# A decoder trunk with split-float32 products: the low part of every third MLP weight tile by an accumulating DMA

## The chip, the cores and the metric

One Trainium2 chip, of which the kernel uses one core. The metric is the time of one execution in device microseconds, the median of the runs shown.

## The reference

The input is x, 256 tokens of 2048 features in float32. Layer 0 is a gated mixer, layer 1 sliding-window attention, and behind each stands an MLP with squared ReLU; every sublayer is followed by a layer norm of alpha times the residual plus its output. What matters here are the two MLPs:

```python
def sq_relu_mlp(x, w_up, w_down):
    return jnp.square(jax.nn.relu(x @ w_up)) @ w_down

# in reference(), for each of the two layers
        x = layer_norm(DEEPNORM_ALPHA * x + mix, ln_g[layer, 0], ln_b[layer, 0])
        x = layer_norm(DEEPNORM_ALPHA * x + sq_relu_mlp(x, mlp_w_up[layer], mlp_w_down[layer]),
                       ln_g[layer, 1], ln_b[layer, 1])
```

w_up is [2048, 8192] and w_down is [8192, 2048], so each MLP reads 128 MiB of weights.

## The kernel before

Every matrix product is done with float32r operands, to float32 accuracy: each operand is a high part (the value rounded to float32r) and a low part (what is left), and a product is the sum of three: high by high, high by low, low by high. All weights of the program stand in one list, in the order of their use, as tiles [128, 1024] of float32, 512 KB each. An MLP has 256 of them (128 of w_up, 128 of w_down): for each quarter of the hidden features 32 tiles of w_up and then 32 of w_down.

The class Weights carries a tile through three stages.

- load() (line 107) and dma() (line 117): SP issues the load of a tile into one of RAW = 4 raw slots, w_raw (line 119). The loads keep the order of the program, so one that waits for its slot holds back all that are behind it.
- ahead() (line 83): a tile that has a place for its parts is split. ScalarE copies raw to w_hi, which rounds it (line 95); VectorE subtracts w_hi from raw and gives w_lo (line 97). Both read the raw slot, and it is free for the load of the tile four further on when both are done. In part of the layer-1 query projection GpSimd does some of the subtractions (by_pool, line 163).
- get() (line 121) and release() (line 130): the products take a tile, and when they are done its place is free. There are SLOTS = 5 places for parts, and EXTRA_SLOTS = 5 more are lent for the time of each MLP (lend(), line 62), ten in all. get() of a tile splits as many tiles ahead as there are places.

The split of a tile and the load behind it are written where a place comes free, so ScalarE, VectorE and SP each follow TensorE through the ring of places. The products are rows_product (line 210: activations stationary, weights moving, 12 matmuls of 512 columns a tile, lines 205 to 207; w_lo is the moving operand of the second of each three) for w_down, and cols_product (weights stationary, lines 246 and 251; w_lo in line 251) for w_up. ScalarE and VectorE also evict the products: in w_up after each four tiles, in w_down after each eight.

A scheduler orders the instructions of each engine by their readiness and adds the semaphore waits; TensorE, ScalarE, VectorE, GpSimd and SP each work through their own list in order.

Of the kernel before, what the change touches and what calls it, by code (L numbers as in the profile page):

```python
# [14 lines left out]
ALU = mybir.AluOpType  # L15
# [16 lines left out]
NEG = -3.0e38  # L32
# [15 lines left out]
class Weights:  # L48
    """The weights in the order of their use: each tile [128, 1024] is loaded and split
    into two float32r parts (high + low = the float32 value) ahead of its products."""  # L50

    def __init__(self, tc, pool, tiles):
        self.tc, self.nc, self.pool, self.tiles = tc, tc.nc, pool, tiles
        self.others, self.by_pool = [], ()
        self.borrowed, self.borrowed_from = [], 0
        self.raw, self.parts, self.held = {}, {}, []
        self.n_raw = self.n_split = self.n_used = 0
        self.free = {"w": SLOTS, "extra": 0}
        self.extra, self.extra_end = None, 0
        self.in_order = False  # L60

    def lend(self, pool, end):
        """More places for the parts of the tiles before number `end`."""
        self.extra, self.extra_end = pool, end
        self.free["extra"] = EXTRA_SLOTS

    def borrow(self, tile, first):
        """Room for the parts of a few tiles from number `first` on, once each."""
        self.borrowed, self.borrowed_from = [(tile[:, i, 0], tile[:, i, 1]) for i in range(4)], first
# [13 lines left out]
    def ahead(self, n_split=None):  # L83
        """Split the tiles that have a place, and load the ones after them."""
        nc = self.nc
        n_split = len(self.tiles) if n_split is None else n_split
        while self.n_split < min(n_split, len(self.tiles)):
            place = self._place(self.n_split)
            if place is None:
                break  # L90
            kind, hi, lo = place
            self.load(self.n_split + 1)
            raw = self.raw.pop(self.n_split)
            for s in self.pieces(self.n_split):
                nc.scalar.copy(out=hi[:, s], in_=raw[:, s])  # L95
                engine = nc.gpsimd if self.n_split in self.by_pool else nc.vector
                sub = engine.tensor_tensor(out=lo[:, s], in0=raw[:, s], in1=hi[:, s].bitcast(F32),  # L97
                                           op=ALU.subtract)
                if self.in_order:
                    self.tc.keep_in_program_order(sub)  # L100
            self.parts[self.n_split] = (hi, lo, kind)
            self.n_split += 1
    def pieces(self, n):
        """The first tile goes in halves, so that the products start early."""
        return [slice(0, TILE // 2), slice(TILE // 2, TILE)] if n == 0 else [slice(0, TILE)]
# [11 lines left out]
    def dma(self, out, in_):  # L117
        """Loads keep the order of the program: what is used first is loaded first."""
        self.tc.keep_in_program_order(self.nc.sync.dma_start(out=out, in_=in_))
# [10 lines left out]
    def release(self):  # L130
        """The oldest tile in use has been used."""
        kind = self.held.pop(0)
        if kind != "borrowed":
            self.free[kind] += 1
# [3 lines left out]
def trunk(ctx: ExitStack, tc: tile.TileContext, t, out):  # L138
    nc = tc.nc
# [13 lines left out]
    ends = {}  # L153
    for name in ("win_v", "win_u", "wout", "mlp0", "kv", "wq", "wo", "mlp1"):
        tiles = (mlp_order(tiles_of("up" + name[3:]), tiles_of("down" + name[3:]))
                 if name.startswith("mlp") else tiles_of(name))
        if name == "wo":
            # the last heads' rows of the first two chunks come after the other rows of both
            tiles = tiles[0:6] + tiles[8:14] + tiles[6:8] + tiles[14:]
# [3 lines left out]
    weights.by_pool = range(ends["kv"] + 4, ends["wq"], POOL_EVERY)  # L163
# [1 line left out]
    ident = const.tile([P, P], F32, name="ident")  # L165
# [21 lines left out]

# [1 line left out]
    def row_steps(stat, apart=False):  # L189
        """[tokens, 512] of both token tiles: activations stationary, weights moving.  # L190
        One step for each weight tile and token tile."""
        if apart:
# [26 lines left out]
    def col_steps(stat, merged=False):  # L219
        """Two blocks [128 features, 256 tokens], transposed: weights stationary. Columns  # L220
        256.. hold the part of the activations' low halves, unless it is merged into the others.
        One step for each weight tile, of both token tiles (tok None); or two, the first with
        the high parts' products of token tile 0."""
        ps = psum.tile([P, 2, 2 * S], F32, tag="mm", name="ps_c")

        def step(i, tok, hi, lo):
            for j in range(4):
                k = 4 * i + j
                for b in range(2):
# [3 lines left out]
                    def high():  # L233
                        if tok is not None:
                            # token tile 0 opens the bank for both
                            part, x = (a.rearrange("p (h t) -> p h t", h=2)[:, :, tok * P:(tok + 1) * P]
# [33 lines left out]
    def skewed(steps, lead, done=None, turn_at=()):  # L270
        """The steps of token tile 0 run `lead` weight tiles ahead of tile 1's; after the
        steps of turn_at, a part of the transposes of a layer norm."""
        held = []
# [16 lines left out]
    def gather_halves(ps, bias=None):  # L290
        """The sum of the two column halves of cols_product (with a bias per feature)."""
        part = work.tile([P, 2, S], F32, tag="part", name="part")
# [9 lines left out]

# [1 line left out]
    def stats_tile():  # L304
# [11 lines left out]
    def norm_rows(acc, stats, g, b, tok, done):  # L316
        """acc = the layer norm of acc, by column chunks; done(chunk) follows each."""
        mu, rstd = moments(stats, tok)
# [18 lines left out]
    def norm_transposed(acc, stats, g, b, xT, tok):  # L337
        """acc = the layer norm of acc, and its transpose goes to xT in parts."""
        def turn(q):
# [9 lines left out]
    def residual(acc, ps, n, stats, scale, toks=range(NT)):  # L349
        """acc = scale * acc + ps on column chunk n."""  # L350
        s = slice(n * 512, (n + 1) * 512)
# [6 lines left out]
    def last_rows(x, stat, stats, scale, norm, norm_turns=True):  # L358
        """The last column chunk before a layer norm: the norm of token tile 0 runs while
        the products of tile 1 do."""  # L360
        ps, steps = row_steps(stat, apart=True)
# [12 lines left out]
    def mlp(x, xT, norm, loads, tags, end):  # L374
        """norm(stats, hT, tok) follows the products of a token tile."""
        stats = stats_tile()
# [32 lines left out]

# [1 line left out]
    cos = const.tile([P, S], F32, name="cos")  # L411
# [4 lines left out]
    sink = const.tile([P, NQH], F32, name="sink")  # L416
    # 0 where key j of the band [previous block | own block] is seen by query i, else NEG
    mask = const.tile([P, 2 * P], F32, name="mask")
# [5 lines left out]

# [1 line left out]
    x = big.tile([P, NT, D], F32, tag="xa", name="x")  # L426
# [107 lines left out]

# [1 line left out]
    with tc.tile_pool(name="attn", bufs=2) as attn:  # L536
# [17 lines left out]

        # keys, transposed, each head's high and low parts in both halves of the partitions;
        # values by rows
        psk, steps = col_steps(xT)
# [18 lines left out]
        for h in range(2):  # L576
            src = kr[h * HD:(h + 1) * HD]
            for other in (h, 1 - h):
# [7 lines left out]
                                in1=bvv.unsqueeze(1).to_broadcast([P, NT, NKV * HD]), op=ALU.add)  # L586
        # [keys, block, kv head, high | low part]
        vp = attn.tile([P, NT, NKV, 2 * HD], F32R, bufs=1, name="vp")
# [4 lines left out]
        def attention(g, qT):  # L593
            """The steps of kv head g: (block of queries, heads, key blocks) at a time."""
            units = [(0, 0, 8, 1), (1, 0, 4, 2), (1, 4, 4, 2)]
# [49 lines left out]
            def values(u):  # L645
                n, h0, nh, nb = units[u]
                pT = st["pT", u].rearrange("p a (r j b) q -> p a r j b q", r=2, b=nb)
                w = nh // 2 * P
                # both parts of the values of the even heads, then of the odd ones
                ps = psum.tile([P, 2, 512], F32, tag="aux", name="ps_o")  # L650
# [31 lines left out]
        for g in range(NKV):  # L682
            # the high and the low parts of a head are 64 partitions each
            qT = attn.tile([P, QPK, S], F32R, tag="qT", bufs=1, name="qT")
# [56 lines left out]
def row_tiles(w):  # L741
    """[K, N] -> [N / 512 * K / 256, 128, 2 * 512]: two K tiles of 512 columns."""
    k, n = w.shape
    return w.reshape(k // 256, 2, P, n // 512, 512).transpose(3, 0, 2, 1, 4).reshape(-1, P, TILE)


def col_tiles(w):
    """[K, N] -> [N / 256 * K / 512, 128, 4 * 256]: four K tiles of 256 columns."""
    k, n = w.shape
# [56 lines left out]
```

## Time and profile before

| | |
|---|---|
| median of 2 runs | 2009.91 us (2007.93 and 2011.89) |
| span of the profiled execution | 2008.3 us |
| TensorE (PE) busy | 1963.9 us, 98% of the span |
| VectorE (DVE) busy | 1252.5 us, 62% |
| ScalarE (ACT) busy | 915.5 us, 46% |
| GpSimd (POOL) busy | 103.1 us, 5% |
| moved by DMA | 377.54 MB |

The profile is of one execution. It gives the span from the first to the last instruction; of what lies around the span it shows nothing, and the runs beside it are from 0.4 us below the span to 3.6 above it. The first MLP lies between about 260 and 970 us of the span, the second between about 1260 and 1960. Busy time of TensorE is from pipelined matmuls whose ends are modelled, so its busy share says that work was always at hand, not how fast it went.

### The profile page before, as it was taken

How to read it: one execution, taken by the hardware profiler on the slowest of the kernel's cores; microseconds unless marked ns; L12 is line 12 of the kernel's file. 1: busy time of each engine (PE TensorE's matmuls, PEld its weight loads, DVE VectorE, ACT ScalarE, POOL GpSimd, SP SyncE). 2: the span in 40 equal slices, each digit the busy share in tenths (PEclk: the TensorE clock that was granted, in tenths of full speed). 3: DMA queues.
4: the chain of work that ended last, by engine and by line, in shares of the span. 5: the costliest groups of instructions: out<-in, count | busy, mean ns of one | idle time of the engine just before them, and what ended most of it. 6: DMA issues, size and time to landing. Idle time of an engine off the chain costs nothing.

```text
span 2008.3 us, 26243 instructions
## 1 busy us (share of the span) xinstructions
PE 1963.9 (98%) x10388; PEld 1685.8 (84%) x10388; DVE 1252.5 (62%) x1345; ACT 915.5 (46%) x1138; POOL 103.1 (5%) x63
## 2 busy tenths in 40 slices
PE   9999999999999999999998889999999999999997
PEld 7888888888888888888898878888888888888886
DVE  5676686555554655564778997965555555555555
ACT  5445445434443443443456675444344344434432
POOL 0000010000000000000133310100000000000001
PEclk9999999999999999999998899999999999999999
DMA  9754846666666666655543336566676666665653
GB/s 339 259 186 151 301 143 214 189 197 224 192 192 191 187 189 194 190 184 166 179 137 107 104 106 227 175 208 190 197 228 187 194 189 189 189 194 185 189 157 104
DMA packets 105963, 377.54 MB, mean 188 GB/s; under 512 B 12272, under 2 KB 12912, under 8 KB 105840
## 3 DMA queue, kind: packets, MB, share of 16 engines
q1 hardware_dynamic: 105840, 375.86, 59.4%
q8 instruction: 81, 1.33, 0.3%
q14 instruction: 42, 0.34, 0.0%
HBM read 373.72 MB, written 2.10 MB: 187 GB/s over the span
## 4 chain that ended last, share of the span: by engine, by line
issue 82%; PE 8%; DVE 6%; ACT 2%; POOL 2%; DMA 0%; SPq 0%; POOLq 0%; ACTq 0%; DVEq 0%
PE ps_r L205 2%; PE ps_r L206 2%; PE ps_r L207 2%; DVE w_lo L97 1%; ACT p L623 1%; PE ps_c L242 1%; PE ps_c L251 1%; DVE x L332 0%; DVE swap L544 0%; POOL rstd L313 0%; DVE pT L186 0%; POOL x L328 0%; POOL x L327 0%; DVE qT L697 0%; DVE x L330 0%
## 5 line engine op out<-in xcount | busy, mean ns | idle before, releaser
L97 DVE TENSOR_TENSOR w_lo<-w_raw,w_hi 128x1024 fp32r<-128x1024 f32 (+1 forms) x655 | 803.9, 1231 | 569.7 <-ACT w_hi L95 567.7
L95 ACT CAST w_hi<-w_raw 128x1024 fp32r<-128x1024 f32 (+1 forms) x669 | 701.3, 1051 | 760.3 <-PE ps_r L207 413.4
L205 PE MATMUL ps_r<-w_hi,hT 128*128 128x512 f32 x1024 | 398.5, 389 | 0.0
L207 PE MATMUL ps_r<-w_hi,hT 128*128 128x512 f32 x1024 | 398.5, 389 | 0.0
L206 PE MATMUL ps_r<-w_lo,hT 128*128 128x512 f32 x1024 | 398.4, 389 | 0.0
L246 PE MATMUL ps_c<-yT,w_hi 128*128 128x512 f32 x960 | 337.1, 398 | 0.0
L246 PE MATMUL ps_c<-oT,w_hi 128*128 128x512 f32 x960 | 337.1, 398 | 0.0
L251 PE MATMUL ps_c<-yT,w_lo 128*128 128x256 f32 x992 | 272.5, 281 | 0.0
L251 PE MATMUL ps_c<-oT,w_lo 128*128 128x256 f32 x992 | 272.5, 281 | 0.0
L207 PEld LDWEIGHTS ps_r<-w_hi,hT 128*128 128x128 f32 x1024 | 192.2, 188 | 40.0
L206 PEld LDWEIGHTS ps_r<-w_lo,hT 128*128 128x128 f32 x1024 | 192.2, 188 | 40.0
L205 PEld LDWEIGHTS ps_r<-w_hi,hT 128*128 128x128 f32 x1024 | 192.2, 188 | 39.5
L246 PEld LDWEIGHTS ps_c<-oT,w_hi 128*128 128x128 f32 x960 | 178.7, 188 | 41.8
L246 PEld LDWEIGHTS ps_c<-yT,w_hi 128*128 128x128 f32 x960 | 178.7, 188 | 41.8
L251 PEld LDWEIGHTS ps_c<-yT,w_lo 128*128 128x128 f32 x992 | 187.4, 189 | 2.7
L251 PEld LDWEIGHTS ps_c<-oT,w_lo 128*128 128x128 f32 x992 | 187.4, 189 | 2.7
L300 DVE TENSOR_TENSOR full<-ps_c,part 128x512 f32<-128x512 f32 x73 | 50.5, 691 | 91.5 <-ACT part L294 83.7
L294 ACT COPY part<-ps_c 128x512 f32<-128x512 f32 x72 | 42.2, 587 | 131.2 <-PE ps_c L246 128.5
L242 PE MATMUL ps_c<-hT,w_hi 128*128 128x256 f32 x512 | 97.8, 294 | 0.0
L313 POOL TENSOR_TENSOR rstd<-ve,half 128x1 f32<-128x1 f32 x10 | 9.9, 987 | 1709.1 <-DVE ve L311 1709.1
L246 PE MATMUL ps_c<-xT,w_hi 128*128 128x512 f32 x256 | 90.2, 396 | 0.0
L242 PEld LDWEIGHTS ps_c<-hT,w_hi 128*128 128x128 f32 x512 | 84.4, 203 | 0.4
(141 smaller groups left out, 2026.4 us busy)
## 6 DMA issues: line engine op xcount, KB each, us to landing
w_raw<-in_up SPq DMA_DIRECT2D x256, 512.0 KB, 4.2
w_raw<-in_down SPq DMA_DIRECT2D x256, 512.0 KB, 4.1
w_raw<-in_win_u SPq DMA_DIRECT2D x32, 512.0 KB, 4.0
w_raw<-in_wout SPq DMA_DIRECT2D x32, 512.0 KB, 4.4
w_raw<-in_wq SPq DMA_DIRECT2D x32, 512.0 KB, 3.6
w_raw<-in_wo SPq DMA_DIRECT2D x32, 512.0 KB, 4.0
w_raw<-in_win_v SPq DMA_DIRECT2D x31, 512.0 KB, 6.2
b_ln_g<-in_ln_g SPq DMA_DIRECT2D x8, 512.0 KB, 5.6
```

What stands on the lines that cost most here:

```text
L95: nc.scalar.copy(out=hi[:, s], in_=raw[:, s])
L97: sub = engine.tensor_tensor(out=lo[:, s], in0=raw[:, s], in1=hi[:, s].bitcast(F32), op=ALU.subtract)
L205: nc.tensor.matmul(out=ps[tok], lhsT=xh, rhs=wh, start=first, stop=False)
L206: nc.tensor.matmul(out=ps[tok], lhsT=xh, rhs=wl, start=False, stop=False)
L207: nc.tensor.matmul(out=ps[tok], lhsT=xl, rhs=wh, start=False, stop=last)
L242: nc.tensor.matmul(out=ps[:, b, 0:S], lhsT=hi[:, w], rhs=stat[:, k, h * S:(h + 1) * S], start=first and h == 0, stop=last and h == 1)
L246: nc.tensor.matmul(out=ps[:, b, :], lhsT=hi[:, w], rhs=stat[:, k, :], start=first, stop=last)
L251: nc.tensor.matmul(out=ps[:, b, 0:S], lhsT=lo[:, w], rhs=stat[:, k, 0:S], start=False, stop=False)
L294: nc.scalar.copy(out=part, in_=ps[:, :, S:])
L300: nc.vector.tensor_tensor(out=full, in0=ps[:, :, 0:S], in1=part, op=ALU.add)
L313: nc.gpsimd.tensor_tensor(out=rstd, in0=ve, in1=half, op=ALU.pow)
L623: nc.scalar.activation(out=p[:, i, :], in_=p[:, i, :], func=AF.Exp, bias=top[:, i:i + 1], accum_out=den[:, i:i + 1])
```

## The change

A set by_dma names every third tile of each MLP, but for the first 40 and the last 40: 59 tiles of each, 118 in all. For these, ScalarE writes the negated value of raw, rounded to float32r, to w_lo (that is minus the high part), and a DMA issued by GpSimd adds the raw tile onto it; the sum is the low part. The VectorE subtraction of these tiles is gone. Comments and docstrings are taken out too, which moves line numbers by six.

```diff
-        self.others, self.by_pool = [], ()
+        self.others, self.by_pool, self.by_dma = [], (), ()
...
             for s in self.pieces(self.n_split):
                 nc.scalar.copy(out=hi[:, s], in_=raw[:, s])
+                if self.n_split in self.by_dma:
+                    nc.scalar.mul(out=lo[:, s], in_=raw[:, s], mul=-1.0)
+                    nc.gpsimd.dma_start(out=lo[:, s], in_=raw[:, s], accum_op=ALU.add)
+                    continue
                 engine = nc.gpsimd if self.n_split in self.by_pool else nc.vector
                 sub = engine.tensor_tensor(out=lo[:, s], in0=raw[:, s], in1=hi[:, s].bitcast(F32),
                                            op=ALU.subtract)
...
     weights.by_pool = range(ends["kv"] + 4, ends["wq"], POOL_EVERY)
+    weights.by_dma = (set(range(ends["wout"] + 40, ends["mlp0"] - 40, 3))
+                      | set(range(ends["wo"] + 40, ends["mlp1"] - 40, 3)))
```

Three places show what moves. The numbers behind a name tell one buffer from the next; DMAHW, DMASW, DVE, PE and Activation in a wait are the semaphores of loads, of DMAs from GpSimd, and of the engines. The first is SP's queue of loads where the range begins, before:

```order
L119 DMA w_raw_3201<-in_down0 128x1024 [waits DMAHW2_49,DVE_49]
L119 DMA w_raw_3223<-in_down0 128x1024 [waits DMAHW3_49,DVE_49]
L119 DMA w_raw_3253<-in_down0 128x1024 [waits DMAHW4_49,DVE_49]
L119 DMA w_raw_3271<-in_down0 128x1024 [waits DMAHW5_49,DVE_49]
L119 DMA w_raw_3289<-in_down0 128x1024 [waits DMAHW6_49,DVE_49]
L119 DMA w_raw_3307<-in_down0 128x1024 [waits DMAHW7_49,DVE_49]
L119 DMA w_raw_3325<-in_down0 128x1024 [waits DMAHW0_49,DVE_49]
L119 DMA w_raw_3343<-in_down0 128x1024 [waits DMAHW1_49,DVE_49]
```

and the same eight loads now:

```order
L123 DMA w_raw_3201<-in_down0 128x1024 [waits DMAHW2_49,DVE_49]
L123 DMA w_raw_3224<-in_down0 128x1024 [waits DMAHW3_49,DMASW0_49,Activation_49]
L123 DMA w_raw_3254<-in_down0 128x1024 [waits DMAHW4_49,DVE_49]
L123 DMA w_raw_3272<-in_down0 128x1024 [waits DMAHW5_49,DVE_49]
L123 DMA w_raw_3291<-in_down0 128x1024 [waits DMAHW6_49,DMASW1_49,Activation_49]
L123 DMA w_raw_3309<-in_down0 128x1024 [waits DMAHW7_49,DVE_49]
L123 DMA w_raw_3327<-in_down0 128x1024 [waits DMAHW0_49,DVE_49]
L123 DMA w_raw_3346<-in_down0 128x1024 [waits DMAHW1_49,DMASW2_49,Activation_49]
```

Every third load waits for an accumulating DMA (DMASW) in the place of a VectorE subtraction. The second place is ScalarE in the same part of the program, before:

```order
L95 CAST w_hi_3267<-w_raw_3179 128x1024 [waits DMAHW5_49,PE_49]
L95 CAST w_hi_3285<-w_raw_3201 128x1024 [waits DMAHW6_49,PE_49,Activation_49]
L95 CAST w_hi_3303<-w_raw_3223 128x1024 [waits DMAHW7_49,PE_49,Activation_49]
L95 CAST w_hi_3321<-w_raw_3253 128x1024 [waits DMAHW0_49,PE_49,Activation_49]
L95 CAST w_hi_3339<-w_raw_3271 128x1024 [waits DMAHW1_49,PE_49,Activation_49]
L95 CAST w_hi_3357<-w_raw_3289 128x1024 [waits DMAHW2_49,PE_49,Activation_49]
```

and now:

```order
L95 CAST w_hi_3268<-w_raw_3179 128x1024 [waits DMAHW5_49,PE_49]
L97 ACTIVATE w_lo_3287<-w_raw_3201 128x1024 [waits DMAHW6_49,PE_49]
L95 CAST w_hi_3286<-w_raw_3201 128x1024 [waits PE_49,Activation_49]
L95 CAST w_hi_3305<-w_raw_3224 128x1024 [waits DMAHW7_49,PE_49,Activation_49]
L95 CAST w_hi_3323<-w_raw_3254 128x1024 [waits DMAHW0_49,PE_49,Activation_49]
L97 ACTIVATE w_lo_3342<-w_raw_3272 128x1024 [waits DMAHW1_49,PE_49]
L95 CAST w_hi_3341<-w_raw_3272 128x1024 [waits PE_49,Activation_49]
```

The negation (ACTIVATE) of every third tile stands ahead of the cast of the same tile, not behind it as in the code. The third place is TensorE at the first tile of the range, before:

```order
L205 MATMUL ps_r_3395<-w_hi_3219,hT_2655 128x512 [waits PE_49]
L206 MATMUL ps_r_3395<-w_lo_3220,hT_2655 128x512
L207 MATMUL ps_r_3395<-w_hi_3219,hT_2655 128x512
L205 MATMUL ps_r_3395<-w_hi_3219,hT_2655 128x512
L206 MATMUL ps_r_3395<-w_lo_3220,hT_2655 128x512
```

and now:

```order
L211 MATMUL ps_r_3398<-w_hi_3219,hT_2655 128x512 [waits PE_49]
L212 MATMUL ps_r_3398<-w_lo_3220,hT_2655 128x512 [waits DMASW0_49]
L213 MATMUL ps_r_3398<-w_hi_3219,hT_2655 128x512
L211 MATMUL ps_r_3398<-w_hi_3219,hT_2655 128x512
L212 MATMUL ps_r_3398<-w_lo_3220,hT_2655 128x512
```

TensorE's order is the same; its first product with the low part waits for the accumulating DMA.

## Rows read from the trace of the kernel before

**Rows 1.** The page: span, and busy time of each engine.

```profile
span 2008.3 us, 26243 instructions
PE 1963.9 (98%) x10388; PEld 1685.8 (84%) x10388; DVE 1252.5 (62%) x1345; ACT 915.5 (46%) x1138; POOL 103.1 (5%) x63
```

**Rows 2.** Busy time by stretches, two of each MLP; columns in the first row.

```profile
core 0: us, PE busy (x) PEld busy (x) DVE busy (x) ACT busy (x) POOL busy (x), PEclk, DMA share, GB/s
500.00:600.00 100.00, 100.00 (x510) 84.90 (x509) 56.31 (x56) 43.15 (x47) 0.00 (x0) 1.00 0.64 190
600.00:700.00 100.00, 100.00 (x517) 85.24 (x516) 55.25 (x55) 43.28 (x47) 0.00 (x0) 1.00 0.63 190
1600.00:1700.00 100.00, 100.00 (x516) 85.19 (x515) 54.46 (x54) 42.70 (x45) 0.00 (x0) 1.00 0.63 190
```

**Rows 3.** Who waited for whom, 300 to 900 us: us, times, longest.

```profile
DVE w_lo L97 <- ACT w_hi L95: 218.6, 144, 1.9
ACT w_hi L95 <- PE ps_r L207: 154.9, 93, 1.7
ACT w_hi L95 <- PE ps_c L246: 105.5, 60, 1.8
...
ACT w_hi L95 <- DMA w_raw<-in_up: 1.4, 1, 1.4
```

**Rows 4.** Timeline of ScalarE: start, us, instruction, idle before it.

```profile
599.50 1.05 ACT L95 CAST w_hi<-w_raw 128x1024 fp32r<-128x1024 f32 x1 [1.66 <-PE ps_r L207]
602.22 1.05 ACT L95 CAST w_hi<-w_raw 128x1024 fp32r<-128x1024 f32 x1 [1.67 <-PE ps_r L207]
```

**Rows 5.** Timeline of VectorE, same stretch.

```profile
597.98 1.22 DVE L97 TENSOR_TENSOR w_lo<-w_raw,w_hi 128x1024 fp32r<-128x1024 f32 x1
600.59 1.23 DVE L97 TENSOR_TENSOR w_lo<-w_raw,w_hi 128x1024 fp32r<-128x1024 f32 x1 [1.39 <-ACT w_hi L95]
```

**Rows 6.** What SP's queue waited for, 300 to 900 us.

```profile
SPq L119 <- DVE w_lo L97: 505.6, 217, 3.5
```

**Rows 7.** DMA queues and issues, 300 to 900 us; the last number is us to landing.

```profile
q1 hardware_dynamic: 32143, 117.00, 64.0%
...
w_raw<-in_up SPq DMA_DIRECT2D x112, 512.0 KB, 4.2
w_raw<-in_down SPq DMA_DIRECT2D x105, 512.0 KB, 4.2
b_ln_g<-in_ln_g SPq DMA_DIRECT2D x2, 512.0 KB, 5.7
b_ln_b<-in_ln_b SPq DMA_DIRECT2D x2, 512.0 KB, 5.4
```

**Rows 8.** Groups by line, 320 to 860 us: busy us, mean ns, idle before.

```profile
L97 DVE TENSOR_TENSOR w_lo<-w_raw,w_hi 128x1024 fp32r<-128x1024 f32 x195 | 238.6, 1224 | 204.0 <-ACT w_hi L95 203.7
L95 ACT CAST w_hi<-w_raw 128x1024 fp32r<-128x1024 f32 x195 | 205.3, 1053 | 248.0 <-PE ps_r L207 154.9 <-PE ps_c L246 88.7 <-PE ps_c L251 4.1
```

**Rows 9.** All loads of line 119, whole span.

```profile
DMA to landing us min/median/max: 2.6/4.2/10.3
```

**Rows 10.** DMA issues of the page; the last number is us to landing.

```profile
w_raw<-in_down SPq DMA_DIRECT2D x256, 512.0 KB, 4.1
...
w_raw<-in_win_v SPq DMA_DIRECT2D x31, 512.0 KB, 6.2
...
lnv_b<-in_lnv_b SPq DMA_DIRECT2D x2, 512.0 KB, 8.9
```

**Rows 11.** Timeline of TensorE in the stretch of rows 4 and 5.

```profile
599.30 0.39 PE L205 MATMUL ps_r<-w_hi,hT 128*128 128x512 f32 x1
599.53 0.39 PE L206 MATMUL ps_r<-w_lo,hT 128*128 128x512 f32 x1
599.75 0.39 PE L207 MATMUL ps_r<-w_hi,hT 128*128 128x512 f32 x1
...
600.89 0.39 PE L206 MATMUL ps_r<-w_lo,hT 128*128 128x512 f32 x1
601.12 0.39 PE L207 MATMUL ps_r<-w_hi,hT 128*128 128x512 f32 x1
601.34 0.39 PE L205 MATMUL ps_r<-w_hi,hT 128*128 128x512 f32 x1
```

## The prediction

> **What bounds the kernel now.** I read the page first, then the busy times by stretches, then who waits for whom in a stretch, and last the timelines of single engines. The page shows TensorE busy for 1963.9 of 2008.3 us, VectorE for 62%, ScalarE for 46%, GpSimd for 5% [rows 1]. The stretches say where the missing 44 us are not: inside both MLPs TensorE is busy 100.00 of 100 us, at a granted clock of 1.00, that is the 2.4 GHz level, and GpSimd executes nothing [rows 2]. So in the stretch that the change touches nothing but TensorE's own pace can be won, and every wait that reaches TensorE is a loss.
>
> The waits of 300 to 900 us, which lie in the first MLP, show the direction: VectorE waits for ScalarE (218.6 us) and ScalarE waits for TensorE (154.9 and 105.5 us), because a split starts when TensorE gives a place back. No TensorE row stands among them, and ScalarE waited for a weight load once, for 1.4 us [rows 3]. ScalarE casts one tile every 2.72 us after 1.67 us of idling [rows 4], and VectorE subtracts 1.23 us right behind [rows 5]. SP waits for that subtraction before nearly every load, 217 times, 505.6 us in all [rows 6]: the raw slot is the only thing that holds a load back. 217 loads in 600 us make 2.765 us a tile.
>
> A load needs 4.2 us from issue to landing [rows 7]. The raw slot comes round after four tiles, 11.1 us; cast, subtraction and load use 1.05 + 1.22 + 4.2 = 6.5 of them [rows 7, 8]. The spare time is 4.6 us a tile. For the finished parts there are ten places, so a part is needed nine tiles, 24.9 us, after its place came free.
>
> **Removed.** 118 subtractions of 1.224 us [rows 8], 144 us of VectorE. No TensorE row waits for VectorE there [rows 3], so this is worth 0.
>
> **Added on ScalarE and GpSimd.** 118 negations of a [128, 1024] tile; the nearest row, the cast of the same shape, has 1.053 us [rows 8]. ScalarE goes from 43% to about 56% busy in these stretches; it idles 1.67 us before each cast, which hides 1.05 us in one tile of three. GpSimd issues the 118 DMAs with nothing else to do [rows 2]. Cost of both: 0, as long as what follows the negation is on time.
>
> **Moved: the release of the raw slot.** This is the term that decides. The order shows the negation ahead of the tile's cast, and the load of tile n+4 waiting for the accumulating DMA of tile n, where it waited for VectorE. Loads are issued in order on SP, so n+5 and n+6, whose slots are long free, wait behind it, and the three then start together. Tile n+6 is again one of every third, so there is a loop of six tiles: the DMA of n lands, three loads start, the third lands, the tile is negated, its own accumulating DMA runs. TensorE takes 6 x 2.765 = 16.6 us for six tiles. If the loop takes longer, the loads set the pace.
>
> Its parts. One load occupies the 16 DMA engines for 600 x 0.64 / 221 = 1.74 us (217 weight loads and four others) [rows 7], so undisturbed the third of three lands after 4.2 + 2 x 1.74 = 7.7 us. The negation is 1.05 us. Call A the time from the negation's end to the release. The loop fits if A stays under 16.6 - 7.7 - 1.05 = 7.8 us.
>
> A stands in no row: before, all moving of tiles is on the hardware queue q1 [rows 7]. Its lower end is that of a load, 4.2 us. Its upper end is the longest time to landing of any load of the kernel, 10.3 us [rows 9]. My value lies between them: 4.2 as for a load, 1.74 more because the old destination is read beside the source, and sharing. Loads that start close together do land late: 6.2 us for the first weights and 8.9 us for a constant, against 4.1 [rows 10]. With loads on the engines 64% of the time, and an accumulation of 2 x 1.74 = 3.5 us of engine time alternating with them, each delays the other by 0.64 x 3.5 = 2.2 us. So A is 8.1 us, the third load lands after 9.9, and the loop takes 9.9 + 1.05 + 8.1 = 19.1 us, 2.5 too long.
>
> By the Trainium skill (DMA: Bandwidth & Descriptors, "Anatomy of one DMA — SWDGE (gpsimd) path") a DMA issued by GpSimd costs about 2.0 us plus its bytes at 436 GB/s, an estimate of 3.2 us for this tile. With A at 3.2 the loop would be 12 us and nothing would be lost. No row here shows a transfer from that queue, so the trace neither bears it out nor refutes it. Another section of the page, "Issuing engines are not separate DMA queues", says that DMAs of all issuers run on the same 16 engines and interleave; that is the sharing above, and without it the loop would be 7.7 + 1.05 + 5.9 = 14.7 us and fit.
>
> **The sum.** Each MLP has 176 tiles in the range, 29.3 loops, so 29.3 x 2.5 = 73 us. The first part of it is paid out of the reserve: low parts come 1.05 + 8.1 = 9.2 us after their place, and are needed at 24.9, so 16 us go by unseen. That leaves 57 us in an MLP and 115 us in both. The profiled execution's span is 2008.3 us; the two runs are 2007.93 and 2011.89, their median 1.6 us above the span, so I add to 2010: 2125 us. What is late then is the raw tile: ScalarE waits for loads, and TensorE for the low parts, in both MLPs.
>
> Bounds. With A at 4.2 and no sharing the loop takes 13 us: 0. With A at 10.3 and the third load delayed by the whole 3.5 us, it takes 11.2 + 1.05 + 10.3 = 22.5, 5.9 too long, 173 - 14 = 159 us in an MLP, some 320 in both: 2330 us. Below nothing the bound is TensorE's own pace (third rival).
>
> **Rivals.** First, all is hidden: the accumulation costs the engines no more than a load and lands within 7.8 us, also beside loads. The loop closes in time, TensorE stays at 100%, and the time is 2010 us, not slower. The point from which it decides is A plus the third load's delay at about 7.8 us; for it speaks the plain load's 4.2 us, against it the second read and the loads that come in bursts. Its place is the SP queue.
>
> Second, the DMA engines become the bound: if one accumulation takes their time of three loads or more, three tiles cost 3 x 1.74 + 5.2 = 10.4 us against 8.3, so 2.1 us too many for 117 groups of three, 252 less 32 of reserve: 2230 us, and by four loads' time 2430. For it speaks that engines are already 64% taken; against it that only bytes read twice are sure, and with 3.5 us they are at 8.7 of 8.3 us, barely over.
>
> Third, TensorE gets faster because VectorE reads less of the memory beside it. Its matmuls of 512 columns start 0.227 us apart, where 512 columns at 2.4 GHz are 0.213. Were the whole 6% VectorE's doing, a third of it over 973 us would give 20 us: 1990 us. But the starts are as far apart before the subtraction of 600.59 us as during it [rows 5, 11], so nothing supports it.
>
> That the change does less than it says can be left out: the order shows 118 DMAs on GpSimd and 118 fewer VectorE instructions.
>
> **How the numbers follow.** A measurement here tells about 2% from no change, 40 us. My forecast, 2050 to 2200 us, has a chance of 0.43; all hidden 0.31; DMA engines as the bound, above 2200, 0.24; faster 0.02. That makes slower 0.67, same 0.31, faster 0.02. The range takes in the first rival and the upper bound from rows, 2004 to 2330 us; what is left out is an accumulation dearer than any load seen. For the forecast alone it is 2050 to 2200.
>
> **What would show it.** In the changed profile the time from issue to landing of the accumulating DMA is A: about 8 us confirms it, under 6 makes the first rival right, above 11 the second. SP should wait mainly for those DMAs, loads should start in threes, ScalarE should wait for loads in the MLPs, and TensorE's busy share there should fall to about 90%. The DMA share should rise from 0.64 to between 0.8 and 1.0. TensorE at 100% in the MLPs, or a DMA share near 0.8 with short landings, makes the forecast wrong.

## The result and the profile after

The changed kernel takes 2063.74 us (median of 2 runs, 2058.64 and 2068.84), the kernel before 2009.91: a ratio of 1.0267 with an interval of 1.0201 to 1.0332, slower by 54 us. The profiled execution has a span of 2056.8 us, 48.5 more than before. The direction and the mechanism of the forecast are there, the size is not: 115 us were forecast.

The page of the changed kernel: span, busy time of the engines, the queue of the accumulating DMAs (packets, MB, share of 16 engines' span), the chain that ended last, and the issues of those DMAs with the median us to landing.

```profile
span 2056.8 us, 26623 instructions
PE 1978.9 (96%) x10388; PEld 1696.1 (82%) x10388; DVE 1107.9 (54%) x1227; ACT 1018.9 (50%) x1256; POOL 205.7 (10%) x181
...
q0 software_dynamic: 16992, 61.87, 16.4%
...
PE 42%; DMA 29%; issue 14%; DVE 8%; ACT 4%; SPq 1%; POOL 1%; ACTq 0%; POOLq 0%; DVEq 0%
...
w_lo<-w_raw POOLq DMA_DIRECT2D x118, 512.0 KB, 7.1
```

VectorE has lost 118 instructions and 145 us, as counted, and ScalarE has gained about 103 us; neither was at its limit [rows 1]. DMA has 29% of the chain that ended last; in the kernel before it had 0%, but 82% of that chain was issue (time in which the profile shows no wait), so the two chains compare only roughly. The accumulating DMA has its own queue, q0. Its 16.4% of 2056.8 us are 337 us of all 16 engines together, 2.86 us for each of the 118. From issue to landing one takes 7.1 us in the median: that is the forecast's A.

Busy time by stretches, columns as in [rows 2]; the first row is the kernel before, the others are the changed kernel:

```profile
400.00:880.00 480.00, 480.00 (x2424) 407.22 (x2423) 264.29 (x258) 204.87 (x216) 0.00 (x0) 1.00 0.64 194
...
400.00:880.00 480.00, 465.92 (x2311) 394.05 (x2310) 181.54 (x187) 239.61 (x254) 47.79 (x55) 0.99 0.87 241
500.00:600.00 100.00, 100.00 (x508) 85.10 (x507) 41.82 (x46) 54.66 (x60) 10.44 (x12) 0.99 0.87 245
600.00:700.00 100.00, 90.81 (x449) 76.86 (x448) 36.26 (x38) 48.26 (x51) 9.57 (x11) 0.97 0.86 236
660.00:680.00 20.00, 13.07 (x64) 11.13 (x63) 6.79 (x7) 9.20 (x11) 1.03 (x2) 0.83 0.91 259
```

The DMA share rose from 0.64 to 0.87. TensorE does not lose a little everywhere: it is busy for 100 us, then loses 9 us in the next 100. The counts of matmuls in such a stretch are no measure of its pace: a tile of w_down has 12 matmuls, all of 512 columns, and a tile of w_up has 16, half of them of 256, so the count depends on which of the two falls into the stretch.

Who waited for whom from 300 to 900 us, then SP's queue in the same stretch (us, times, longest):

```profile
ACT w_hi L95 <- DMA w_raw<-in_up: 117.2, 61, 6.5
ACT w_hi L95 <- DMA w_raw<-in_down: 83.9, 42, 6.3
ACT w_lo L97 <- DMA w_raw<-in_down: 26.6, 18, 4.0
ACT w_lo L97 <- DMA w_raw<-in_up: 20.8, 11, 4.3
ACT w_hi L95 <- PE ps_c L252: 20.3, 12, 1.8
PE ps_c L252 <- DVE full L306: 12.4, 4, 6.9
```

```profile
SPq L123 <- DMA w_lo<-w_raw: 311.1, 59, 9.7
SPq L123 <- DVE w_lo L101: 150.7, 71, 3.5
```

Before, ScalarE waited for TensorE (154.9 and 105.5 us) and only once for a load [rows 3]. Now it waits for loads, in all 248.5 us in these four rows, and hardly for TensorE: the tiles come late and the ring of places is no longer what sets its pace. SP, which waited for VectorE alone [rows 6], waits 59 times for the accumulating DMAs, once for each in this MLP. That is the turn that the forecast described.

The loop itself can be read from the first and the last of this MLP's 59 accumulating DMAs (timeline of GpSimd: start, us, instruction, idle before it), with the negation ahead of one between them on ScalarE:

```profile
374.64 1.05 POOL L98 DMA_DIRECT2D w_lo<-w_raw  x1 [86.08 <-ACT w_lo L97]
...
603.43 1.06 ACT L97 ACTIVATE w_lo<-w_raw 128x1024 fp32r<-128x1024 f32 x1 [3.77 <-DMA w_raw<-in_down]
604.79 0.87 POOL L98 DMA_DIRECT2D w_lo<-w_raw  x1 [10.03 <-ACT w_lo L97]
...
889.92 0.87 POOL L98 DMA_DIRECT2D w_lo<-w_raw  x1 [12.28 <-ACT w_lo L97]
```

58 intervals in 515.28 us are 8.88 us for three tiles, 17.8 for six. TensorE's pace before was 16.6 for six. So a loop is 1.2 us too long, where 2.5 were forecast. Over 29 loops that is 515.3 - 29 x 16.6, 34 us.

The loads of the eight tiles behind the first MLP (line, first and last start) tell what of the 34 us came through; first the kernel before, then the changed one:

```profile
L119 SPq DMA_DIRECT2D w_raw<-in_kv x8: 327/328/328, 971.5 to 984.5; - x8
```

```profile
L123 SPq DMA_DIRECT2D w_raw<-in_kv x8: 327/328/328, 995.3 to 1007.9; - x8
```

23.8 us of the 34 reach the end of the MLP, so 10 us were taken out of the reserve. TensorE tells the same: with its matmuls matched one by one against those of the kernel before, it falls back by 24.3 us in the first MLP and by 24.4 in the second, together about the span's 48.5.

### The profile page after: what moved, and what is told of

It reads as the page before. It is cut to its first block, busy times and chain, and to the rows that moved or that the text cites. A ratio compares the mean times of both kernels' runs of the same rounds, so it can differ in the third digit from the quotient of the medians.

```text
span 2056.8 us, 26623 instructions
## 1 busy us (share of the span) xinstructions
PE 1978.9 (96%) x10388; PEld 1696.1 (82%) x10388; DVE 1107.9 (54%) x1227; ACT 1018.9 (50%) x1256; POOL 205.7 (10%) x181
## 3 DMA queue, kind: packets, MB, share of 16 engines
q0 software_dynamic: 16992, 61.87, 16.4%
## 4 chain that ended last, share of the span: by engine, by line
PE 42%; DMA 29%; issue 14%; DVE 8%; ACT 4%; SPq 1%; POOL 1%; ACTq 0%; POOLq 0%; DVEq 0%
PE ps_c L252 13%; DMA w_lo<-w_raw 12%; DMA w_raw<-in_down 9%; PE ps_c L257 8%; DMA w_raw<-in_up 8%; PE ps_r L211 6%; PE ps_r L212 6%; PE ps_r L213 6%; DVE w_lo L101 2%; PE ps_c L248 1%; ACT w_hi L95 1%; SPq L123 1%; ACT w_lo L97 1%; DVE x L338 1%; ACT p L629 1%
## 5 line engine op out<-in xcount | busy, mean ns | idle before, releaser
L101 DVE TENSOR_TENSOR w_lo<-w_raw,w_hi 128x1024 fp32r<-128x1024 f32 (+1 forms) x537 | 659.2, 1233 | 789.5 <-ACT w_hi L95 785.7
L252 PE MATMUL ps_c<-oT,w_hi 128*128 128x512 f32 x960 | 345.0, 404 | 16.2 <-DVE full L306 8.6
L252 PE MATMUL ps_c<-yT,w_hi 128*128 128x512 f32 x960 | 344.3, 403 | 17.0 <-DVE full L306 12.4
L212 PEld LDWEIGHTS ps_r<-w_lo,hT 128*128 128x128 f32 x1024 | 192.2, 188 | 39.9
L98 POOL DMA_DIRECT2D w_lo<-w_raw x118 | 102.8, 871 | 1103.7 <-ACT w_lo L97 1085.3
L97 ACT ACTIVATE w_lo<-w_raw 128x1024 fp32r<-128x1024 f32 x118 | 124.9, 1059 | 110.1 <-DMA w_raw<-in_down 60.8
```

The lines of the kernel that those rows point to most:

```text
L97: nc.scalar.mul(out=lo[:, s], in_=raw[:, s], mul=-1.0)
L98: nc.gpsimd.dma_start(out=lo[:, s], in_=raw[:, s], accum_op=ALU.add)
L212: nc.tensor.matmul(out=ps[tok], lhsT=xh, rhs=wl, start=False, stop=False)
L252: nc.tensor.matmul(out=ps[:, b, :], lhsT=hi[:, w], rhs=stat[:, k, :], start=first, stop=last)
```

## The experiments

The prediction's own theory (the loop: an accumulating DMA holds a raw slot, SP's queue of loads stands behind it, and the third of the loads closes the loop too late) stood against one rival: the 16 DMA engines have too much to move, wherever the accumulations are put and whoever waits for them. Each experiment below is the changed kernel with one edit, unless it says otherwise. Ratios are to the kernel before on the same chip. Where a run loses nothing, that is read from the row 400 to 880 us, columns as in [rows 2]. Matched one by one, the matmuls of each of these runs keep their distance from those of the kernel before to 0.01 us, from 360 us to 985.

**A plain copy in place of the accumulation.** The copy writes the raw tile over the negated one. The kernel leaves out the forming of these 118 low parts: their products are done with the raw values.

```diff
-                    nc.gpsimd.dma_start(out=lo[:, s], in_=raw[:, s], accum_op=ALU.add)
+                    nc.gpsimd.dma_start(out=lo[:, s].bitcast(F32), in_=raw[:, s])
```

> Theory 1 (the loop raw slot, SP queue, third load, negation, accumulating DMA of six tiles is longer than TensorE's 16.6 us): a plain DMA of the same tile on the same queue reads half as much, so it should land in 5 to 6 us in the place of 7.1; the loop is then about 9.0 + 1.4 + 5.5 = 15.9 us, it fits, and the time is 2010 to 2020 us. Theory 2 (any transfer on GpSimd's queue beside the loads costs this, by its bytes on the DMA engines): the bytes written are the same 62 MB, the time stays at 2050 us or above. The low parts of 118 tiles are not formed: the raw tile is copied over them.

2010.14 us, ratio 0.9997 (0.9988 to 1.0006). The stretch, the landing and the queue from 400 to 880 us:

```profile
400.00:880.00 480.00, 480.00 (x2424) 407.26 (x2423) 197.99 (x203) 255.57 (x271) 29.60 (x55) 1.00 0.74 256
...
DMA to landing us min/median/max: 2.8/5.7/8.8
...
q0 software_dynamic: 8064, 29.36, 15.3%
```

Same queue, same semaphores, same holds, and nothing is lost. The negation, the issue on GpSimd and the wait as such are therefore free; what costs is the longer accumulation. The 15.3% of 480 us are 73 us for 56 copies, 1.31 us each, where an accumulation takes 2.86: 2.2 times as much. Both theories can live with this run, since the copy is shorter and also lighter.

**Every fourth and every sixth tile** (88 and 60 DMAs in place of 118; the diff is that of every fourth, the other has a 6).

```diff
-    weights.by_dma = (set(range(ends["wout"] + 40, ends["mlp0"] - 40, 3))
-                      | set(range(ends["wo"] + 40, ends["mlp1"] - 40, 3)))
+    weights.by_dma = (set(range(ends["wout"] + 40, ends["mlp0"] - 40, 4))
+                      | set(range(ends["wo"] + 40, ends["mlp1"] - 40, 4)))
```

> 88 accumulating DMAs in the place of 118. Theory 1: with four raw slots the same slot is accumulated each time, so the loop closes in four tiles: first load 4.6 + negation 1.4 + DMA 6.5 to 7.1 = 12.5 to 13.1 us against 4 x 2.765 = 11.1; 44 loops an MLP, 62 to 90 us, less about 9 of reserve, in both MLPs 105 to 160: 2115 to 2170 us, slower than with every third tile though fewer are moved. Theory 2 (time by the number of DMAs): three quarters of the loss, about 2050 us.

> Every sixth tile, 60 accumulating DMAs (30 in each MLP). Theory 1: one loop of six tiles and not two interleaved, so nothing else accumulates while the three loads run: third load 7.7 to 8.5, negation 1.4, DMA 6 to 7, in all 15.1 to 16.9 against 16.6 us: 2010 to 2020 us. Theory 2 (time by the number of DMAs): half the loss, about 2036 us.

2011.14 us, ratio 1.0001 (0.9992 to 1.001), and 2012.46 us, ratio 1.0007 (0.9998 to 1.0016). With every sixth tile the loop theory's 2010 to 2020 us came, and not the 2036 of a loss that goes by the number of DMAs. With every fourth tile I had expected a loss by either theory, and there is none. Every fourth tile, the stretch, and the time to landing of line 98:

```profile
400.00:880.00 480.00, 480.00 (x2425) 407.27 (x2424) 213.25 (x217) 241.67 (x257) 35.60 (x41) 1.00 0.78 240
...
DMA to landing us min/median/max: 4.5/4.9/9.6
```

With step four, tile n+4 is itself one of the set: the loop is one of four tiles, and the load in it is the first behind the wait. Load and accumulation then take turns in a single chain, with little beside them, and A is 4.9 us. With the first load at some 3.6 us, the negation to the DMA's issue at 1.4 and 0.1 of hand-overs the loop is 10 us, and TensorE needs 11.1. The theory's links hold, and one of its numbers is wrong: A nearly alone is 4.9, where the forecast had 5.9.

**The engines' work without the hold**, on the kernel before: all subtractions stay on VectorE, and every third tile's high part is added by an accumulating DMA onto a scratch tile that nobody reads. No raw slot waits for it.

```diff
-SLOTS = 5
+SLOTS = 4
...
+                if self.n_split in self.by_dma:
+                    nc.gpsimd.dma_start(out=self.sums[self.n_split % 2], in_=hi.bitcast(F32),
+                                        accum_op=ALU.add)
...
```

> The kernel before with its VectorE subtractions, and besides them an accumulating DMA of 512 KB for every third tile in the same ranges, from the finished high part into a scratch tile: the DMA engines get the same work, but no raw slot and no product waits for it. (Nine places for parts in the place of ten make room for the scratch.) Theory 1: loads land somewhat later, 4.4 to 5 us, but in time: 2010 to 2020 us. Theory 2 (bytes on the DMA engines): 2050 us or more.

2016.25 us, ratio 1.0032 (1.0019 to 1.0045).

```profile
400.00:880.00 480.00, 480.00 (x2422) 407.15 (x2422) 265.44 (x259) 205.09 (x215) 48.66 (x56) 1.00 0.93 256
...
sums<-w_hi POOLq DMA_DIRECT2D x118, 512.0 KB, 6.6
```

The DMA share is 0.93, above the changed kernel's 0.87, and TensorE does not lose a microsecond in this stretch. The rival is refuted for the change: with every third tile accumulated the engines can move all of it. The 6 us come in ahead of the accumulations: the matmuls, matched one by one with those of the kernel before, are 1.1 us late from 310 us on and 6.1 from 1330 on, and nothing is added while the accumulations run (379 to 860 us and 1385 to 1866). That the one place less for parts causes this is likely; no run tested it by itself.

**The same 118 DMAs, with a shorter loop.** Twice: the accumulated tiles get two raw slots of their own, out of the same four; or six raw slots in place of four, with one place for parts less.

```diff
-            raw = self.pool.tile([P, TILE], F32, tag="w_raw", bufs=RAW, name="w_raw")
+            n = self.n_raw
+            near = [i in self.by_dma for i in (n, n - 1, n - 2)]
+            own = near[0] if any(near) else n % 2
+            raw = self.pool.tile([P, TILE], F32, tag=f"w_raw{int(own)}", bufs=RAW // 2, name="w_raw")
```

```diff
-RAW = 4
-SLOTS = 5
+RAW = 6
+SLOTS = 4
```

> All 118 accumulating DMAs; still four raw slots, but two of them belong to the accumulated tiles and two to the others, so that the load that waits for an accumulating DMA is that of tile n+6, and not of n+4. Theory 1 (the hold of the raw slot ahead of SP's queue): the DMA has six tiles, 16.6 us, less load and negation, to land, and holds nobody back: 2010 to 2020 us. Theory 2 (bytes on the DMA engines): the same bytes at the same rate, 2050 us or more.

> The changed kernel with six raw slots (and nine places for parts, to make room). Theory 1: the load that waits is that of tile n+6, the first of its burst, so the loop is 4.6 + 1.4 + 7.1 = 13.1 us or less against 16.6: 2010 to 2020 us. Theory 2: 2050 us or more.

2009.69 us, ratio 0.9991 (0.9982 to 1.0001), and 2008.91 us, ratio 0.9994 (0.9984 to 1.0003). Own slots, the stretch and what SP's queue waited for in it:

```profile
400.00:880.00 480.00, 480.00 (x2424) 407.18 (x2423) 198.08 (x203) 256.05 (x271) 47.80 (x55) 1.00 0.89 256
...
SPq L126 <- DVE w_lo L101: 331.6, 117, 5.7
SPq L126 <- DMA w_lo<-w_raw: 25.9, 24, 4.2
```

Six raw slots, the same, and last what SP waited for in the changed kernel in this stretch:

```profile
400.00:880.00 480.00, 480.00 (x2422) 407.13 (x2421) 197.88 (x203) 257.51 (x271) 48.66 (x56) 1.00 0.90 257
...
SPq L123 <- DMA w_lo<-w_raw: 337.5, 57, 10.4
...
SPq L123 <- DMA w_lo<-w_raw: 282.7, 54, 9.1
```

In both, the tile whose load waits for the DMA of tile n is n+6 itself, so its load is the first behind the wait and not the third. (By the semaphores in the traces this holds for 58 and 46 of the 59 tiles of the first MLP. With six slots it is n+7 for the other 13, and n+6 does not wait for that DMA.) That one link is enough: the same DMAs, the same engine time, and the whole 54 us are gone. With six raw slots SP waits even longer for the accumulating DMAs than in the changed kernel (337.5 us against 282.7 in the same stretch), and an accumulation takes 7.8 us there. So neither the length of SP's wait nor A alone decides, but whether the chain from release to release closes in TensorE's time.

**The same count and the same links, in another phase.** Tiles 0 and 1 of each six are accumulated, not 0 and 3. The third load behind tile 1 still closes the loop.

```diff
-    weights.by_dma = (set(range(ends["wout"] + 40, ends["mlp0"] - 40, 3))
-                      | set(range(ends["wo"] + 40, ends["mlp1"] - 40, 3)))
+    weights.by_dma = {n + i for i in range(2) for first, end in (("wout", "mlp0"), ("wo", "mlp1"))
+                      for n in range(ends[first] + 40, ends[end] - 40, 6)}
```

> Still two accumulated tiles of every six, 118 or 120 DMAs in all, but neighbours (tiles 0 and 1 of six, in the place of 0 and 3). Theory 1 with sharing (two loops set against each other by three tiles: the accumulations of the one lie on the three loads of the other, which makes the third load 9.3 and the DMA 7.1 us): the two accumulations lie together and the loads follow together, third load about 5.5, negation 1.4, DMA 6 to 7 us: 13 to 14 of 16.6 us, 2010 to 2020 us. Theory 1b (the hold alone, whatever overlaps): the loop has the same links as in the changed kernel, 2050 us or more. Theory 2 (bytes on the DMA engines): 2050 us or more.

2011.77 us, ratio 0.9997 (0.9988 to 1.0007), with 120 DMAs of 5.9 us in the median:

```profile
400.00:880.00 480.00, 480.00 (x2423) 407.22 (x2422) 196.89 (x202) 257.89 (x272) 48.80 (x56) 1.00 0.90 257
...
w_lo<-w_raw POOLq DMA_DIRECT2D x120, 512.0 KB, 5.9
```

A lost 1.2 us, as much as the changed kernel's loop is too long by, and the loss is gone. It is not A alone: followed tile by tile in the first MLP, the third load lands 7.4 us behind the release where it was 8.7, and its negation starts 2.1 us later where it was 0.5, so the loop now has time to spare. The reading is that with 0 and 3 two loops run half a turn apart, and an accumulation of the one falls beside the three loads of the other, while with 0 and 1 the two accumulations stand together, with fewer loads beside them.

**Every second tile** (176 DMAs; the diff is that of every fourth tile with a 2).

> 176 accumulating DMAs in the place of 118, two loops of four tiles each (raw slots 0 and 2). Alone each would take 3.6 + 1.4 + 5.0 = 10.0 us against 11.1, as with every fourth tile; interleaved, loads and accumulations overlap as in the changed kernel, 4.6 + 1.4 + 7.1 = 13.1 or more, and the engines are full (2 x 1.6 + 2.9 = 6.1 of 5.5 us in two tiles). Theory 1 with sharing: 44 x 2.0 - 9 = 80 us an MLP or more, 2170 to 2300 us. Theory 2 (by the number of DMAs): one and a half times the loss, 2090 us.

2095.02 us, ratio 1.0412 (1.0391 to 1.0433). Behind the first MLP, and the queues from 400 to 880 us:

```profile
L123 SPq DMA_DIRECT2D w_raw<-in_kv x8: 327/328/328, 1011.4 to 1024.1; - x8
...
q1 hardware_dynamic: 23328, 84.95, 48.8%
q0 software_dynamic: 11349, 41.31, 46.8%
```

The loop theory's expectation was missed, and 2090, the loss by the number of DMAs, was met. The run doesn't rehabilitate the rival for the change itself, since the runs above hold, but at this density both bounds are near: the queues fill the engines to 96%, and at these shares two tiles cost 0.956 x 480 us x 2 / 162 loads, 5.7 us, where TensorE takes 5.5; and the loop (first load 5.2, accumulation 5.5, 1.4 and 0.1) is 12.2 us for four tiles, where TensorE takes 11.1. This run can't tell the two apart.

**Another queue for the loads that wait**: GpSimd issues them, so that SP's queue is free.

```diff
             for s in self.pieces(self.n_raw):
+                if self.n_raw - RAW in self.by_dma:
+                    self.nc.gpsimd.dma_start(out=raw[:, s], in_=self.tiles[self.n_raw][:, s])
+                    continue
```

> All 118 accumulating DMAs stay; the loads that wait for them are issued by GpSimd, behind the DMA that they wait for, so that the other loads on SP's queue are not held back. Theory 1: the loop of six tiles is cut, since tile n+6 no longer waits behind tile n+4; one slot alone needs 4.6 + 1.4 + 7.1 once and about 7 twice in twelve tiles, 27 of 33 us: 2010 to 2020 us. Theory 2 (bytes on the DMA engines): as many bytes, 2060 us or more.

2143.91 us, ratio 1.0633 (1.0579 to 1.0688): much worse than the change itself. What GpSimd waited for, 400 to 880 us:

```profile
POOL w_raw L116 <- ACT w_lo L97: 162.8, 19, 11.1
POOL w_raw L116 <- DVE w_lo L101: 97.5, 16, 10.7
POOL w_raw L116 <- DMA w_lo<-w_raw: 59.3, 9, 9.2
```

GpSimd is in order as well. The load of tile n+4 now waits there for DMA n, and the accumulating DMA of tile n+3 stands behind the load. The rows put most of these waits down to ScalarE and VectorE, whose semaphores the load waits for too. But by the landings in the trace 49 of the first MLP's 59 such loads start within 0.7 us behind the landing of an accumulating DMA. The hold was moved onto the queue that must release it, so the run says nothing about SP's hold, only that such a wait must not share a queue with the work that ends it.

**The changed kernel once more**, for the scatter of its loss.

> The changed kernel once more, word for word, beside the kernel before on one chip, for a narrower interval: 2050 to 2075 us by every theory.

2067.24 us (2051.12 to 2076.58 over 4 runs), ratio 1.025 (1.0201 to 1.0299). Its profile has a span of 2074.8 us, accumulating DMAs of 7.6 us, and these first and last starts and first load behind the MLP:

```profile
374.73 1.05 POOL L98 DMA_DIRECT2D w_lo<-w_raw  x1 [86.10 <-ACT w_lo L97]
...
900.13 0.87 POOL L98 DMA_DIRECT2D w_lo<-w_raw  x1 [7.36 <-ACT w_lo L97]
...
L123 SPq DMA_DIRECT2D w_raw<-in_kv x8: 327/328/328, 1005.3 to 1019.8; - x8
```

A loop is 525.4 / 29 = 18.1 us here, 44 us too long in the MLP, and 33.8 of them come through.

## Why the prediction was right in kind and wrong in size

**Right.** Subtractions off VectorE were worth nothing; negations and issues cost nothing (the plain copy shows it, with 2010.14 us). The loss comes out of the raw slot's release, through SP's in-order queue; the runs that shorten only this loop lose nothing, and moving the same bytes without the hold loses nothing while they are moved. The time to landing, 7.1 us, lies between the 6 and 11 that were to tell the rivals apart, SP waits mainly for those DMAs, ScalarE for loads, and the DMA share is 0.87, in the band named. TensorE's busy share did not fall to about 90%: it is 97% from 400 to 880 us (465.92 of 480).

**The step that failed: "the loop takes 9.9 + 1.05 + 8.1 = 19.1 us, 2.5 too long".** It takes 17.8 us and is 1.2 too long. The excess is a small difference of two large sums, so small errors decide it:

- A was 8.1 and is 7.1. Its unshared part was 5.9 and is 4.9, the median where only every fourth tile is accumulated. Sharing was 2.2 and is 2.1 to 2.2, if the 4.9 and the 5.0 us of every sixth tile are taken as the unshared part. The engine time was 3.5 us, twice a load's 1.74, and is 2.86.
- The third load was to land after 9.9 us; what is left of 17.8 for it is 17.8 - 7.1 - 1.4 - 0.1, some 9.2. Followed tile by tile in the trace, the third load lands 8.7 us behind the release in the mean, and its negation starts 0.5 us later (for some tiles ScalarE does the cast first). That "the three then start together" holds in 23 of the 59 cases of this MLP (starts within 1 us of one another). SP waits for VectorE too, for the other slots. And by the semaphores the load that waits for the DMA of tile n is that of n+4 for 45 of the 59 tiles and that of n+5 for 14, where n+6 is the second behind the wait.
- The negation was 1.05; from its start to the DMA's issue it is 1.36 (603.43 to 604.79), 0.3 more.

Together that is 1.0 + 0.7 - 0.3 = 1.4 us too much, about the 1.3 between 2.5 and 1.2.

**The reserve was mis-sized too, the other way.** "16 us go by unseen" counted the ten places for parts. The runs agree on about 10 us: 34 late and 23.8 through, 44 and 33.8, and for every second tile 531.2 us from first to last start against 481, so 50 late and 39.9 through (971.5 to 1011.4). Where GpSimd issues the loads that wait, 79 us late give 70 through. With the measured terms the forecast's sum is 2 x (34 - 10), 48 us, against 48.5 in the profile; as the 10 comes from these runs, its support is that it comes out alike in them.

The two errors pull opposite ways: the forecast's 73 us with the reserve of 10 would have given 126 us, and the measured 34 with the reserve of 16 only 36. That the time still lies in the forecast's range, 2050 to 2200 us, is in part luck.

Why 10 and not 16, the timelines of the engines at the worst stall suggest (ScalarE, VectorE, TensorE):

```profile
672.48 1.04 ACT L95 CAST w_hi<-w_raw 128x1024 fp32r<-128x1024 f32 x1 [5.19 <-DMA w_raw<-in_up]
673.43 0.58 ACT L300 COPY part<-ps_c 128x512 f32<-128x512 f32 x1
...
673.55 1.23 DVE L101 TENSOR_TENSOR w_lo<-w_raw,w_hi 128x1024 fp32r<-128x1024 f32 x1 [7.97 <-ACT w_hi L95]
674.70 0.68 DVE L306 TENSOR_TENSOR full<-ps_c,part 128x512 f32<-128x512 f32 x1
...
675.43 0.79 PE L252 MATMUL ps_c<-yT,w_hi 128*128 128x512 f32 x1 [6.93 <-DVE full L306]
676.24 0.63 PE L252 MATMUL ps_c<-yT,w_hi 128*128 128x512 f32 x1
676.88 0.63 PE L252 MATMUL ps_c<-yT,w_hi 128*128 128x512 f32 x1
...
680.46 0.40 PE L252 MATMUL ps_c<-yT,w_hi 128*128 128x512 f32 x1
680.81 0.40 PE L252 MATMUL ps_c<-yT,w_hi 128*128 128x512 f32 x1
```

TensorE waits here neither for a low part nor for an accumulating DMA. It waits for the eviction of an earlier product. ScalarE's half of that (673.43 us) stands behind a cast that waited 5.19 us for a load, and VectorE's half (674.70) stands behind the subtraction of the same tile. What TensorE waited for in the MLPs of the changed kernel, and one row of the changed kernel run once more:

```profile
PE ps_c L252 <- DVE full L306: 21.0, 7, 6.9
PE ps_c L252 <- DVE x L359: 12.2, 4, 6.9
...
PE ps_r L212 <- DMA w_lo<-w_raw: 4.5, 3, 2.2
```

Both rows of the changed kernel are evictions, in w_up and in w_down. Their 33.2 us and the 15.0 us by which TensorE's busy time grew make 48.2 of the span's 48.5. So the forecast's "TensorE for the low parts" was wrong in the main: the profiled execution shows no such wait, and the other run has four, 6.0 us in all, beside 37.9 us for evictions. The lateness reaches TensorE mostly through the evictions, which come every four tiles in w_up and are due before the parts are. That this cuts the reserve to 10 us is read from the order of these rows; no run tested it by itself.

**The rivals.** The DMA engines as the bound: A would have passed 11 us, and it would have needed the engine time of three loads, 5.2 us, where one has 2.86, and the run without the hold carried a share of 0.93 at no cost while the accumulations ran. All hidden: it failed by 1.2 us in 16.6, and pairs of tiles or two own slots bring it about. TensorE faster: in the runs without a loss as many subtractions are off VectorE, and between 360 and 985 us TensorE's matmuls gain not 0.01 us by it.

By the Trainium skill (DMA: Bandwidth & Descriptors, "Anatomy of one DMA — SWDGE (gpsimd) path") the estimate for this DMA was 3.2 us. The runs decide against it: the shortest accumulating DMA of any run landed after 4.5 us, and the plain copies have 5.7 in the median beside loads, 2.8 at the least. By the Trainium skill (DMA: Bandwidth & Descriptors, "Issuing engines are not separate DMA queues") DMAs of all issuers run on the same 16 engines and interleave. With that the runs agree: 4.9 us nearly alone, 7.1 beside the other loop's loads.

No version here beats the kernel before. The MLPs are bound by TensorE, so the variants without a loss only give VectorE time that nobody needs.

## What to carry to other kernels

When a buffer's release is handed to a slower agent, write down the whole ring from release to release, with every transfer that starts behind the wait on the same in-order queue, and compare it with the consumer's time for that many tiles; here 1.2 us in 16.6 cost 2.7% of the kernel, and putting the waiting load first behind the wait, or the buffers into a ring of their own, cost nothing. An excess that is a small difference of long chains should carry a wide range, down to nothing. And lateness can come out where the in-order engines meet, and not where the late data are used: here it was the eviction behind the late split.

## What the runs showed that was not expected

An accumulating DMA of 512 KB within the chip's SBUF keeps the 16 engines for 2.86 us (2.72 with every fourth tile, 3.40 in the run without the hold), against 1.31 for the plain copy on the same queue; nearly alone it lands after 4.9 us.

The engine time of a load is not fixed, as the forecast took it: it was 1.74 us before [rows 7], and with every second tile accumulated 48.8% of 480 us for 162 loads are 1.45 us. So the engine times counted in one run do not simply add up to the share of another.

After the longest wait of the first MLP TensorE runs at the 1.2 GHz level of its clock: from 675.43 us on, after 6.93 us of waiting, like matmuls start 0.64 us apart (676.24, 676.88), and from 680.46 on 0.35 (680.81). The stretch from 660 to 680 us has a granted clock of 0.83, and 675 to 680 has 0.50. Not every wait is followed by this: after the 2.27 us before 657.17 like matmuls start 0.35 us apart at once. TensorE's busy time grew by 15 us for the same 10388 matmuls. In the runs that lost time the loss in the MLP is the loop's lateness less some 10 us, so no loss by the clock beside it shows; whether the slower matmuls only fill time in which the next tile would have been late anyway, no run separates.
